# RMSNorm and matmul: half of the weights loaded ahead of x, and square roots for four tiles at a time

## The chip, the cores and the metric

The kernel runs on one core of one Trainium2 chip. The metric is the device time of one execution in microseconds (us); a median of several runs is given with its lowest and highest. A run has a state: "slow" where it is over 1.5% above the fastest of the same kernel, else "fast"; only fast runs are compared.

The engines: PE multiplies matrices, ACT (ScalarE), DVE (VectorE) and POOL (GpSimd) do the elementwise work, SP issues the transfers, and 16 DMA engines carry them. A transfer is split over the 16; I call the share that one engine has to carry its **ring**.

## The reference

```python
def reference(x, gamma, weight, eps):          # x 16 x 1024 x 512, weight 512 x 768, all float32
    rms = np.sqrt(np.mean(x ** 2, axis=-1, keepdims=True) + eps)
    x_norm = x / rms * gamma
    return np.matmul(x_norm, weight).astype(np.float32)
```

## The kernel before

The 16,384 rows are 128 tiles of 128 rows; two tiles are a pair. POOL casts a tile to bf16, PE transposes it (as 32-bit words, two bf16 each), DVE evacuates the transposes to SBUF, PE multiplies with the weights (four steps k, each 512 and 256 columns wide), and ACT and DVE alternate in scaling the result by 1/rms on its way to the output. ACT also squares x and sums the squares (`square`), and takes the root (`root`); DVE inverts it. Weights are scaled by gamma once and cast to bf16.

```python
    def root(i, n, ssq):
        rms = stats.tile([P, 4], F32, name="rms")
        nc.scalar.activation(out=rms[:, :n], in_=ssq[:, :n], func=AF.Sqrt, scale=1.0 / D, bias=eps_sb)
        rstd = stats.tile([P, 4], F32, name="rstd")
        nc.vector.reciprocal(out=rstd[:, :n], in_=rms[:, :n])
        ...
    def norms(i, n):
        ssq = stats.tile([P, 4], F32, name="ssq")
        for t in range(n):
            square(i + t, ssq[:, t:t + 1])
        root(i, n, ssq)
    ...
        touched = singles.tile([P, 2, 1], F32)
        nc.scalar.dma_start(out=touched, in_=wv[:, :, 0:1])      # one word of each weight row
        ...
        load_until(2)            # x tiles 0 and 1
        load_weights(0)          # weights for k = 0, 1
        load_until(3)            # x tile 2
        load_weights(1)          # weights for k = 2, 3
        load_until(2 * XG)       # x up to tile 31
        for _ in range(20):
            nc.sync.drain()
        ...
        warm_up(6)               # dummy matmuls, before the first data
        cast(0, nc.vector)
        square(0, ssq[:, 0:1])
        ...                      # gamma
        cast(1, nc.vector)
        square(1, ssq[:, 1:2])
        transpose_tile(0)
        warm_up(2)
        transpose_tile(1)
        warm_up(5)
        ...                      # weights 0 and 1 scaled, tiles 0 to 2 with k = 0, 1, then k = 2, 3
        for j in range(2, NP):
            load_until(2 * j + AHEAD)
            if j + 3 < NP:
                cast(2 * j + 6, nc.gpsimd, 2)
            if j + 1 < NP:
                norms(2 * j + 2, 2)
            ...                  # matmuls of pair j, transposes of a later pair in between
```

Outputs are stored eight tiles at a time in the middle, in smaller pieces at both ends; the last tile in two pieces (512 and 256 columns).

Of the kernel before, what the change touches and what calls it, by code (L numbers as in the profile page):

```python
# [12 lines left out]
F32 = mybir.dt.float32  # L13
# [5 lines left out]
def kernel(  # L19
# [8 lines left out]
    nc = tc.nc  # L28
    P = 128

    x = x.flatten_outer_dims()
    out = out.flatten_outer_dims()
# [4 lines left out]
    NP = NT // 2  # L37
# [27 lines left out]
    singles = ctx.enter_context(tc.tile_pool(name="singles", bufs=1))  # L65
# [3 lines left out]
    stats = ctx.enter_context(tc.tile_pool(name="stats", bufs=4))  # L69
# [2 lines left out]
    opsum = ctx.enter_context(tc.tile_pool(name="opsum", bufs=3, space=bass.MemoryType.PSUM))  # L72
    outp = ctx.enter_context(tc.tile_pool(name="out", bufs=3))

    x_tiles, xb_tiles, tp_tiles, rstd_of, xT_tiles, o_tiles = {}, {}, {}, {}, {}, {}

    def held(tiles, group, i, n=1):
        return tiles[i // group][:, i % group:i % group + n, :]

    def load(i):  # L80
        if i // XG not in x_tiles:
            x_tiles[i // XG] = xin.tile([P, XG, D], F32, name="xt")
        nc.sync.dma_start(out=held(x_tiles, XG, i, x_size[i]), in_=rows(x, i, x_size[i]))  # L83
# [3 lines left out]
    def load_until(i):  # L87
        while starts and starts[0] < i:
            load(starts.pop(0))

    def cast(i, engine, n=1):
        if i // 2 not in xb_tiles:
            xb_tiles[i // 2] = xbp.tile([P, 2, D], BF16, name="xb")
        engine.tensor_copy(out=xb_tiles[i // 2][:, i % 2:i % 2 + n, :], in_=held(x_tiles, XG, i, n))  # L94

    def square(i, ssq):
        jk = junk.tile([P, D], BF16, name="jk")
        nc.scalar.activation(out=jk, in_=held(x_tiles, XG, i)[:, 0, :], func=AF.Square, accum_out=ssq)  # L98
# [7 lines that stand above are left out]
            rstd_of[i + t] = rstd[:, t:t + 1]  # L106

    def norms(i, n):
        ssq = stats.tile([P, 4], F32, name="ssq")
        for t in range(n):  # L110
            square(i + t, ssq[:, t:t + 1])
        root(i, n, ssq)



    def transpose_word(j, t, h):
        if j not in tp_tiles:
            tp_tiles[j] = tpsum.tile([P, 2, 2, P], F32, name="tp")
        words = xb_tiles[j].rearrange("p a d -> p (a d)").bitcast(F32)
        lo = t * (D // 2) + h * P  # L120
        nc.tensor.transpose(out=tp_tiles[j][:, t, h, :], in_=words[:, lo:lo + P], identity=ident_f)  # L121

    def evac(j, t=0, n=2):
        if j not in xT_tiles:
            xT_tiles[j] = xt_pool.tile([P, 2, 2, P, 2], BF16, name="xT")
        src = tp_tiles.pop(j).rearrange("p t h m -> p t (h m)").bitcast(BF16)
        dst = xT_tiles[j].rearrange("p t h m c -> p t (h m c)")
        nc.vector.tensor_copy(out=dst[:, t:t + n, :], in_=src[:, t:t + n, :])  # L128


    def transpose_tile(i):
        for h in range(2):
            transpose_word(i // 2, i % 2, h)
        evac(i // 2, i % 2, 1)
# [7 lines left out]
    def accumulator():  # L142
        return opsum.tile([P, 2, WIDE], F32, name="ops").rearrange("p a b -> p (a b)")
# [16 lines left out]
    def matmuls(i, acc, ks, feed=None):  # L160
        for k in ks:
            matmul(i, k, acc, 0, WIDE)
            if feed:
                feed()
            matmul(i, k, acc, WIDE, O)
# [18 lines left out]
        return feed  # L184

    with tc.manual_schedule():

        wv = weight.rearrange("(h w c) o -> w h (c o)", w=P, c=2)
        touched = singles.tile([P, 2, 1], F32)
        nc.scalar.dma_start(out=touched, in_=wv[:, :, 0:1])  # L190
        g_row = singles.tile([2, P, 2], F32)
        nc.scalar.dma_start(out=g_row, in_=gamma.rearrange("(h w c) -> h w c", w=P, c=2))
        nc.scalar.preload_act_table(AF.Sqrt)  # L193
        w_f32 = singles.tile([P, K, O], F32)

        def load_weights(h):
            nc.sync.dma_start(out=w_f32[:, 2 * h:2 * h + 2, :].rearrange("p c o -> p (c o)"), in_=wv[:, h, :])  # L197

        load_until(2)
        load_weights(0)  # L200
        load_until(3)
        load_weights(1)
        load_until(2 * XG)

        for _ in range(20):
            nc.sync.drain()


        warm = singles.tile([P, WIDE], BF16)
        nc.vector.memset(warm, 0.0)  # L210
        eps_sb = singles.tile([P, 1], F32)
        nc.vector.memset(eps_sb, float(eps))  # L212
        ident_f = singles.tile([P, P], F32)
        make_identity(nc, ident_f)
        spare = accumulator()

        def warm_up(n):
            for _ in range(n):
                nc.tensor.matmul(out=spare[:, :WIDE], lhsT=warm[:, :P], rhs=warm, start=True, stop=True)  # L219

        w_bf = singles.tile([P, K, O], BF16)

        def weights(k, engine, lo=0, hi=O):
            scale(engine, w_bf[:, k, lo:hi], w_f32[:, k, lo:hi], g_sb[:, k % 2, k // 2:k // 2 + 1])


        ssq = stats.tile([P, 4], F32, name="ssq")
        warm_up(6)
        cast(0, nc.vector)
        square(0, ssq[:, 0:1])  # L230
        gp = tpsum.tile([P, 2, 2], F32, name="tp")
        for c in range(2):
            nc.tensor.transpose(out=gp[:, c, :], in_=g_row[:, :, c], identity=ident_f[:2, :2])  # L233
        g_sb = singles.tile([P, 2, 2], F32)
        nc.vector.tensor_copy(out=g_sb, in_=gp)  # L235
        cast(1, nc.vector)
        square(1, ssq[:, 1:2])
        transpose_tile(0)
        warm_up(2)
        transpose_tile(1)  # L240
        warm_up(5)
        acc = [accumulator() for _ in range(4)]
        weights(0, nc.vector, 0, WIDE)
        weights(0, nc.vector, WIDE, O)
        weights(1, nc.scalar)
        cast(2, nc.gpsimd)
        square(2, ssq[:, 2:3])
        matmuls(0, acc[0], [0, 1])
        transpose_tile(2)
        matmuls(1, acc[1], [0, 1])  # L250
        matmuls(2, acc[2], [0, 1])
        weights(2, nc.vector)
        root(0, 3, ssq)
        weights(3, nc.scalar)
        cast(3, nc.gpsimd)
        matmuls(0, acc[0], [2, 3])
        finish_tile(0, acc[0], nc.scalar)
        matmuls(1, acc[1], [2, 3])
        transpose_tile(3)
        finish_tile(1, acc[1], nc.vector)  # L260
        norms(3, 1)
        cast(4, nc.gpsimd)
        cast(5, nc.gpsimd)
        matmuls(2, acc[2], [2, 3])
        finish_tile(2, acc[2], nc.scalar)
        matmuls(3, acc[3], [0, 1, 2, 3], feeder([2], [0, 2, 2, 0], alone=True))
        finish_tile(3, acc[3], nc.vector)
        cast(6, nc.gpsimd, 2)
        cast(8, nc.gpsimd, 2)
        norms(4, 2)  # L270


        one, two, both = [1, 1, 0, 1, 1, 0, 0, 0], [1, 0, 1, 0, 1, 0, 1, 0], [1, 1, 1, 1, 1, 1, 1, 1]
        for j in range(2, NP):
            load_until(2 * j + AHEAD)
            if j + 3 < NP:
                cast(2 * j + 6, nc.gpsimd, 2)
            if j + 1 < NP:
                norms(2 * j + 2, 2)
            if j == NP - 1:  # L280
                break
            if j < 4:
                feed = feeder([j + 1], one)
            elif j == 4:
                feed = feeder([5, 6], both)
            elif j + 2 < NP:
                feed = feeder([j + 2], two)
            else:
                feed = None
            for i, engine in ((2 * j, nc.scalar), (2 * j + 1, nc.vector)):  # L290
                a = accumulator()
                matmuls(i, a, range(K), feed)
                finish_tile(i, a, engine)



        for i in (NT - 2, NT - 1):
            for lo, hi, engine in ((0, WIDE, nc.scalar), (WIDE, O, nc.vector)):
                a = accumulator()
                for k in range(K):  # L300
                    matmul(i, k, a, lo, hi)
                scale(engine, out_tile(i)[:, lo:hi], a[:, lo:hi], rstd_of[i])
                if i == NT - 1:
                    nc.sync.dma_start(out=rows(out, i, 1)[:, 0, lo:hi], in_=out_tile(i)[:, lo:hi])
            if i < NT - 1:
                store(i)
# [35 lines left out]
```

## Time and profile before

| | before |
|---|---|
| time, 3 runs | 211.19 us (211.04 to 211.26) |
| span of the profiled run | 209.6 us |
| second half of the weights lands | 11.45 us |
| first matmul on x | 9.55 us |
| PE starts tile 6 | 19.57 us |
| last output scale starts | 204.58 us |
| SP's last wait, for the stores | 2.7 us |

The last scale frees the last store, and SP waits until all stores have landed. The prediction shows the page, the chain of work and two stretches. Two further lines of the same page: PE's granted clock in the 40 slices (tenths of full speed), and the group of the roots (line, engine, operation, shapes, count, then busy us and mean ns, then idle time before).

```profile
PEclk9999999999999999999999999999999999999997
...
L102 ACT ACTIVATE rms<-ssq,eps_sb 128x2 f32<-128x2 f32 (+1 forms) x64 | 18.9, 296 | 2.1
```

64 roots take ACT 18.9 us.

### The profile page before, as it was taken

The page shows a single profiled execution, that of the slowest core. Times are in us where ns is not written, and L with a number is a line of the kernel's source. Part 1 is how long each engine was busy: PE and PEld are TensorE (multiplying, and loading weights), DVE is VectorE, ACT ScalarE, POOL GpSimd, SP SyncE. Part 2 cuts the span into 40 slices and gives each one's busy share as a digit, 9 for nine tenths or more (in the row PEclk, how much of TensorE's full clock was granted, in tenths as well). Part 3 has the DMA queues.
Part 4 walks back from the last instruction along what each step waited for, and adds up shares of the span by engine and source line. Part 5 has one row for each costly group of instructions (what it writes and reads, how often), then busy time and mean ns, then how long its engine had stood idle before and what let it go on. Part 6 is the DMA issues. An engine that isn't in the chain of part 4 may idle for free.

```text
span 209.6 us, 3586 instructions
## 1 busy us (share of the span) xinstructions
PE 199.2 (95%) x1270; PEld 137.7 (66%) x1295; DVE 111.5 (53%) x204; ACT 158.4 (76%) x388; POOL 65.8 (31%) x71
## 2 busy tenths in 40 slices
PE   7599999999999999999999999999999999999990
PEld 3256766677666776667766667666776666766650
DVE  2256566446545654564465456546645654565450
ACT  5279778877877787788778777877887787778750
POOL 1156533305323072313433044320732126330000
PEclk9999999999999999999999999999999999999997
DMA  6999999999999999999999999999999999799896
GB/s 207 364 431 421 432 399 441 416 391 444 427 444 422 430 427 430 449 417 421 416 450 438 416 433 427 436 435 407 441 427 433 430 433 425 310 399 422 347 383 236
DMA packets 7350, 85.69 MB, mean 409 GB/s; under 512 B 1058, under 2 KB 1188, under 8 KB 3748
## 3 DMA queue, kind: packets, MB, share of 16 engines
q1 hardware_dynamic: 7056, 85.46, 96.9%
q8 instruction: 10, 0.16, 0.3%
q14 instruction: 8, 0.07, 0.1%
q10 hardware_dynamic: 276, 0.00, 0.1%
HBM read 35.13 MB, written 50.33 MB: 408 GB/s over the span
## 4 chain that ended last, share of the span: by engine, by line
PE 88%; DMA 4%; ACT 3%; DVE 1%; issue 1%; SPq 1%
PE ops L156 75%; PE tp L121 13%; DMA w_f<-in_weight_dram 4%; ACT jk L98 1%; ACT ot L138 1%; SPq L83 1%; ACT rms L102 0%; DVE xT L128 0%; DVE w_bf L140 0%; DVE ot L140 0%; SPq L197 0%; DVE rstd L104 0%
## 5 line engine op out<-in xcount | busy, mean ns | idle before, releaser
L156 PE MATMUL ops<-w_bf,xT 128*128 128x512 bf16 (+1 forms) x999 | 192.8, 324 | 4.1 <-DVE w_bf L140 2.5
L156 PEld LDWEIGHTS <-xT 128*128 128x128 bf16 x1024 | 100.0, 98 | 59.3 <-issue 3.2
L94 POOL CAST xb<-xt 128x1024 bf16<-128x1024 f32 (+1 forms) x65 | 65.1, 1015 | 121.6 <-PE tp L121 68.0
L128 DVE COPY xT<-tp 128x1024 bf16<-128x1024 bf16 (+1 forms) x67 | 44.7, 667 | 82.1 <-PE tp L121 81.8
L138 ACT ACTIVATE ot<-ops,rstd 128x768 f32<-128x768 f32 (+1 forms) x65 | 58.1, 894 | 37.5 <-PE ops L156 36.7
L98 ACT ACTIVATE jk<-xt 128x512 bf16<-128x512 f32 x128 | 78.8, 619 | 0.5 <-DMA xt<-in_x_dram 0.5
L121 PE MATMUL tp<-ident_f,xb 128*128 128x128 f32 x256 | 69.2, 274 | 0.1
L140 DVE TENSOR_SCALAR ot<-ops,rstd 128x768 f32<-128x768 f32 (+1 forms) x65 | 64.5, 992 | 2.8 <-PE ops L156 2.8
L121 PEld LDWEIGHTS tp<-ident_f,xb 128*128 128x128 f32 x256 | 36.1, 142 | 3.7 <-PE tp L121 0.3
L98 ACT ACTIVATION_READ_ACCUMULATOR jk<-xt 128x1 f32 x128 | 24.4, 191 | 0.0
L102 ACT ACTIVATE rms<-ssq,eps_sb 128x2 f32<-128x2 f32 (+1 forms) x64 | 18.9, 296 | 2.1
L104 DVE RECIPROCAL rstd<-rms 128x2 f32<-128x2 f32 (+1 forms) x64 | 9.9, 155 | 2.1 <-ACT rms L102 2.0
L219 PE MATMUL ops<-warm 128*128 128x512 bf16 x13 | 5.0, 534 | 1.2 <-DVE eps_sb L212 1.2
L138 ACT ACTIVATE w_bf<-w_f,g_sb 128x768 bf16<-128x768 f32 x2 | 1.9, 935 | 4.6 <-DMA w_f<-in_weight_dram 4.6
L219 PEld LDWEIGHTS <-warm 128*128 128x128 bf16 x13 | 1.5, 124 | 2.7 <-DVE eps_sb L212 1.2
L140 DVE TENSOR_SCALAR w_bf<-w_f,g_sb 128x512 bf16<-128x512 f32 (+2 forms) x3 | 1.4, 485 | 2.9 <-DMA w_f<-in_weight_dram 2.9
L193 ACT ACT_TABLE_LOAD x1 | 1.3, 1283 | 1.8 <-issue 1.8
L94 DVE CAST xb<-xt 128x512 bf16<-128x512 f32 x2 | 0.8, 423 | 2.4 <-DMA xt<-in_x_dram 2.4
L233 PEld LDWEIGHTS tp<-ident_f,g_row 2*128 2x128 f32 x2 | 0.3, 202 | 0.8 <-issue 0.8
L210 DVE MEMSET warm<- 128x256 uint32 x1 | 0.3, 272 | 0.9 <-PEq L323 0.9
L233 PE MATMUL tp<-ident_f,g_row 2*128 2x2 f32 x2 | 0.4, 264 | 0.0
L235 DVE COPY g_sb<-tp 128x4 f32<-128x4 f32 x1 | 0.2, 163 | 0.3 <-PE tp L233 0.3
(7 smaller groups left out, 1.0 us busy)
## 6 DMA issues: line engine op xcount, KB each, us to landing
out_dram<-ot SPq DMA_DIRECT2D x12, 3072.0 KB, 16.1
xt<-in_x_dram SPq DMA_DIRECT2D x5, 4096.0 KB, 20.2
xt<-in_x_dram SPq DMA_DIRECT2D x3, 2048.0 KB, 18.0
out_dram<-ot SPq DMA_DIRECT2D x4, 1536.0 KB, 10.2
xt<-in_x_dram SPq DMA_DIRECT2D x4, 1024.0 KB, 13.2
out_dram<-ot SPq DMA_DIRECT2D x4, 768.0 KB, 9.1
out_dram<-ot SPq DMA_DIRECT2D x7, 384.0 KB, 10.1
w_f<-in_weight_dram SPq DMA_DIRECT2D x2, 768.0 KB, 8.1
```

The costliest lines, as they stand in the source:

```text
L83: nc.sync.dma_start(out=held(x_tiles, XG, i, x_size[i]), in_=rows(x, i, x_size[i]))
L94: engine.tensor_copy(out=xb_tiles[i // 2][:, i % 2:i % 2 + n, :], in_=held(x_tiles, XG, i, n))
L98: nc.scalar.activation(out=jk, in_=held(x_tiles, XG, i)[:, 0, :], func=AF.Square, accum_out=ssq)
L102: nc.scalar.activation(out=rms[:, :n], in_=ssq[:, :n], func=AF.Sqrt, scale=1.0 / D, bias=eps_sb)
L104: nc.vector.reciprocal(out=rstd[:, :n], in_=rms[:, :n])
L121: nc.tensor.transpose(out=tp_tiles[j][:, t, h, :], in_=words[:, lo:lo + P], identity=ident_f)
L128: nc.vector.tensor_copy(out=dst[:, t:t + n, :], in_=src[:, t:t + n, :])
L138: nc.scalar.mul(out=dst, in_=src, mul=r)
L140: nc.vector.tensor_single_scalar(out=dst, in_=src, scalar=r, op=mybir.AluOpType.mult)
L156: nc.tensor.matmul(out=acc[:, lo:hi], lhsT=xT_tiles[i // 2][:, i % 2, k // 2, :, k % 2], rhs=w_bf[:, k, lo:hi], start=(k == 0), stop=(k == ...
L193: nc.scalar.preload_act_table(AF.Sqrt)
L219: nc.tensor.matmul(out=spare[:, :WIDE], lhsT=warm[:, :P], rhs=warm, start=True, stop=True)
```

## The change

The intent is to have PE start on x earlier, by putting half of the weights first in the queue, and to take load off ACT and DVE by one root and one reciprocal for four tiles. The small read of one word per weight row goes, the casts of tiles 0 and 1 move from DVE to POOL, and seven dummy matmuls become three.

```diff
+    def norms_by_four(j):
+        if j % 2:
+            norm_sums[j] = stats.tile([P, 4], F32, name="ssq")
+        ssq = norm_sums[j - (j + 1) % 2]
+        for t in range(2):
+            square(2 * j + t, ssq[:, 2 * (1 - j % 2) + t:2 * (1 - j % 2) + t + 1])
+        if j % 2 == 0:
+            root(2 * j - 2, 4, ssq)
+        elif j == NP - 1:
+            root(2 * j, 2, ssq)
...
-        touched = singles.tile([P, 2, 1], F32)
-        nc.scalar.dma_start(out=touched, in_=wv[:, :, 0:1])
...
-        load_until(2)
         load_weights(0)
         load_until(3)
         load_weights(1)
...
         warm_up(6)
-        cast(0, nc.vector)
-        square(0, ssq[:, 0:1])
...
-        cast(1, nc.vector)
-        square(1, ssq[:, 1:2])
-        transpose_tile(0)
-        warm_up(2)
-        transpose_tile(1)
-        warm_up(5)
...
-        cast(2, nc.gpsimd)
-        square(2, ssq[:, 2:3])
+        warm_up(3)
+        for i in range(3):
+            cast(i, nc.gpsimd)
+            square(i, ssq[:, i:i + 1])
+        transpose_tile(0)
+        transpose_tile(1)
...
-            if j + 1 < NP:
+            if j < 4:
                 norms(2 * j + 2, 2)
+            for ahead in ([5, 6] if j == 4 else [j + 2] if 4 < j < NP - 2 else []):
+                norms_by_four(ahead)
```

More of the change, by code (lines that the diff above doesn't have):

```diff
@@ L73 @@
     outp = ctx.enter_context(tc.tile_pool(name="out", bufs=3))
-    x_tiles, xb_tiles, tp_tiles, rstd_of, xT_tiles, o_tiles = {}, {}, {}, {}, {}, {}
+    x_tiles, xb_tiles, tp_tiles, rstd_of, xT_tiles, o_tiles, norm_sums = {}, {}, {}, {}, {}, {}, {}
     def held(tiles, group, i, n=1):
@@ L186 @@
     with tc.manual_schedule():
-        wv = weight.rearrange("(h w c) o -> w h (c o)", w=P, c=2)
-        touched = singles.tile([P, 2, 1], F32)
-        nc.scalar.dma_start(out=touched, in_=wv[:, :, 0:1])
         g_row = singles.tile([2, P, 2], F32)
@@ L193 @@
         nc.scalar.preload_act_table(AF.Sqrt)
+        wv = weight.rearrange("(h w c) o -> w h (c o)", w=P, c=2)
         w_f32 = singles.tile([P, K, O], F32)
```

## The prediction

> **What bounds the kernel now.** I read the page first: busy shares, then the 40 slices, then the chain. After that I read the chain and the timeline of the first 20 us, the two stretches where the change acts, and POOL's waits in the middle.
>
> The page of the kernel before (busy time of each engine; then, in 40 slices of 5.24 us, PE and the DMA engines; then the chain that ended last):
>
> ```profile
> span 209.6 us, 3586 instructions
> PE 199.2 (95%) x1270; PEld 137.7 (66%) x1295; DVE 111.5 (53%) x204; ACT 158.4 (76%) x388; POOL 65.8 (31%) x71
> ...
> PE   7599999999999999999999999999999999999990
> ...
> DMA  6999999999999999999999999999999999799896
> ...
> PE ops L156 75%; PE tp L121 13%; DMA w_f<-in_weight_dram 4%; ACT jk L98 1%; ACT ot L138 1%; SPq L83 1%; ACT rms L102 0%; DVE xT L128 0%; DVE w_bf L140 0%; DVE ot L140 0%; SPq L197 0%; DVE rstd L104 0%
> ```
>
> TensorE is 9 in every slice but the first two and the last. 88% of the chain is its matmuls and transposes. DMA is also full, from slice 2 to slice 34. ACT is at 76% and on the chain only in the opening. So there are three parts: an opening, a long stretch that PE sets with DMA close behind it, and a tail.
>
> The chain in order of time shows the opening:
>
> ```profile
> 2.58 8.87 DMA w_f<-in_weight_dram
> 11.45 0.02 issue
> 11.47 0.63 DVE w_bf L140
> 12.11 0.04 issue
> 12.15 0.82 PE ops L156 x4
> 12.97 0.02 issue
> 13.00 0.90 ACT ot L138
> ...
> 18.43 0.30 ACT rms L102
> ...
> 18.76 0.04 DVE rstd L104
> 18.80 0.05 issue
> 18.84 0.68 DVE xT L128
> 19.52 0.05 issue
> 19.57 0.39 PE ops L156
> ```
>
> The second half of the weights is issued at 2.58 and lands at 11.45; that alone is the chain until then. ACT carries it from 13.00 to 18.73. From 19.57, where PE starts tile 6, the chain is PE. The period of one tile read off that chain (for example 26.58, 28.86, 30.38, 31.89) is 1.52 us. 122 tiles x 1.5185 us = 185.3, and 19.57 + 185.3 = 204.8; PE's last matmuls end at 204.56. So after 19.57 PE loses nothing. The last output scale and the last store then make 209.6, a tail of 5 us. **The change can alter the end only by moving the 19.57, or by putting a stall into the PE stretch.**
>
> DMA: a tile takes 256 KiB in and 384 KiB out, 655,360 bytes per 1.5185 us = 432 GB/s. The slices of the middle move 391 to 450, mostly 420 to 440. DMA is thus just at its limit at PE's pace. How much room there is shows in POOL's casts (start, time, idle before and what ended it):
>
> ```profile
> 123.31 3.99 POOL L94 CAST xb<-xt 128x1024 bf16<-128x1024 f32 x4 [8.25 <-DMA xt<-in_x_dram]
> 147.53 3.99 POOL L94 CAST xb<-xt 128x1024 bf16<-128x1024 f32 x4 [8.17 <-DMA xt<-in_x_dram]
> ```
>
> The load of tiles 80 to 95 lands at 123.31. Its first cast (1.04 us) ends at 124.35. PE transposes tile 80 while it computes tile 76, which starts at 19.57 + 70 x 1.5185 = 125.9. The room is some 1.6 us; the same sum for tile 96 gives 1.6. PE can't run more than about 1.6 us earlier unless these loads land earlier too.
>
> [...] most engines end the first half of the weights by 5.8 us, but four of the 16 stall for some 2.7 us at their first weight packets (single packets of 1.1 to 1.7 us against a median of 0.234 us, and pauses before them), so it lands only at 9.0. The same four are still behind at the second half, whose last packet ends at 11.05. [...] Here the first dummy matmuls come every 0.43 us and the last five in 1.24 us together, and 2.5 us of idle before the first real matmul at 9.55 didn't cool it. [...]
>
> **The change part by part.**
>
> (1) Order of the loads. Ahead of the end of the second half lie the same bytes as before: three x tiles (16 KiB per ring each) and two weight halves (48 KiB per ring each). From packets: 3 x 8 x 0.082 + 2 x 8 x 0.232 = 5.7 us per ring. Started at 1.75 that is 7.4; add a first-packet delay of 0.4, the four rings' stall of 2.7 and some 0.5 of smaller delays: 11.0, which is what was seen. Order alone doesn't change that sum. If the stall stays, the second half lands at 11.0 to 11.5 again: gain 0 to 0.4. If it goes (it came just as the small reads of one word per weight row, which are removed, had passed through the same rings, so they could be its cause), the gain is up to 2.7.
>
> (2) First matmul. Half 0 should land at 4.5 (no stall) to 7 (stall), x tile 0 0.7 later; then a POOL cast 0.62, transposes 0.43, evacuation 0.42: first matmul at 7 to 8.7 instead of 9.55. But PE had finished everything that half 0 allows, tiles 0 to 2 with k = 0 and 1, just before 12.15: it waited only some 0.25 us there. An earlier start without an earlier second half turns into waiting: gain at most 0.25.
>
> (3) The casts of tiles 0 and 1 go from DVE (0.42 us each) to POOL (0.62 us). Seven dummy matmuls become three. All lies before the second half lands: 0 on the path.
>
> (4) Roots by four. In the 57 pairs from tile 10 on, 62 roots over two become about 34 over four: some 28 ACTIVATEs of 0.296 = 8.3 us off ACT, 28 reciprocals of 0.155 = 4.3 us off DVE. ACT waits 36.7 us for PE in total, so this comes off idle time: 0. Squares come one pair (3.04 us) earlier and free x buffers earlier, but a load already queues behind issued stores (packets of the load issued at 54.29 start 4 us later), so landing isn't issue-bound: about 0.
>
> (5) A cost: at tile 8 the change puts four squares ahead of one root, to get two pairs ahead. ACT there before:
>
> ```profile
> 22.21 0.62 ACT L98 ACTIVATE jk<-xt 128x512 bf16<-128x512 f32 x1
> ...
> 23.57 0.30 ACT L102 ACTIVATE rms<-ssq,eps_sb 128x2 f32<-128x2 f32 x1
> 24.56 0.90 ACT L138 ACTIVATE ot<-ops,rstd 128x768 f32<-128x768 f32 x1 [0.69 <-PE ops L156]
> ```
>
> Four squares of 0.81 from 22.21 end at 25.45, the root at 25.78, the reciprocal at 25.95. DVE works in order, and in its order the evacuation of pair 5 stands behind that reciprocal: it moves from 24.45 to 25.97 and ends at 26.66. PE wants that pair for tile 10 at 26.1: a stall of about 0.6 us. Later pairs have nothing of the kind (odd ones have no root, even ones the old order).
>
> Sum: stall stays: 211.2 - 0.3 + 0.6 = 211.5. Stall goes: 211.2 - 2.6 + 0.6 = 209.2.
>
> **The rivals.** (a) The weight stall vanishes with the small reads: 209.2. For it: its timing. Against it: those reads look like a deliberate warm-up of the weights' addresses. (b) Without that warm-up, all 16 rings stall at the cold weights, and longer: half 2 lands perhaps 1 us later, 212.5. For it: first x packets also took 0.2 to 0.58 us instead of 0.08. [...] (d) PE starts earlier but x loads don't: stalls near 120 us and later give back all beyond 1.6 us: 210.2. (e) ACT is the true bound and the roots give back 8 us: against it, ACT's 36.7 us of waiting for PE and PE's gapless stretch; I give it 2%.
>
> **Range and chances.** I weigh "stall stays" 0.45, "goes, in whole or part" 0.35, "worse" 0.2: near 0.45 x 211.5 + 0.35 x 209.8 + 0.2 x 212.6 = 211.1. I say 211.0, range 208.9 to 212.9. Faster by over 2% needs 207.0, below even the best sum: 0.02. Slower by over 2% needs 215.4: 0.03.
>
> **What would show it.** The landing of the second half (11.45 before) and the start of tile 6 (19.57 before) should move by nearly the same amount, and the span with them, plus a gap of 0.6 us on PE before tile 10 with DVE's evacuation as its releaser. The PE stretch should keep 1.5185 us per tile; ACT's busy time should fall by some 8 us without effect. The prediction is wrong if PE shows gaps in the middle (DMA), if its clock drops in the opening, or if the period of a tile changes.

The forecast came to 0.45 x 211.5 + 0.35 x 209.8 + 0.2 x 212.6 = 211.1 and was put at 211.0. That the small reads are a warm-up, and that without them the second half lands 1 us later (rival b), were guesses that no trace shows; in e3, without the reads, it landed at 11.38. That DMA is at its limit is read from its share, 0.99 from 20 to 200 us.

## The result, and the profile after

The changed kernel took 210.83 us (210.49 to 211.55, six runs), the kernel before in the same rounds 211.12 us (210.89 to 211.67, six runs). The ratio of after to before is 0.9986, with a 95% interval of 0.9966 to 1.0007: the same, within 2%. A ratio is the mean time of one kernel's fast runs over the mean of the other's fast runs of the same rounds, so it isn't quite the ratio of the two medians.

The page after (the lines that answer to those of before):

```profile
span 209.2 us, 3496 instructions
PE 200.1 (96%) x1266; PEld 137.5 (66%) x1291; DVE 109.0 (52%) x173; ACT 149.5 (71%) x359; POOL 67.1 (32%) x73
...
PEclk9889999999999999999999999999999999999997
DMA  6999999999999999999999999999999999699886
...
PE ops L168 77%; PE tp L133 13%; DMA xt<-in_x_dram 3%; ACT jk L98 1%; ACT ot L150 1%; ACT rms L102 0%; SPq L83 0%; DVE xT L140 0%; POOL xb L94 0%; DVE ot L152 0%; SPq L206 0%; DVE rstd L104 0%
...
L102 ACT ACTIVATE rms<-ssq,eps_sb 128x4 f32<-128x4 f32 (+3 forms) x35 | 10.4, 297 | 1.1
```

ACT is busy 149.5 us instead of 158.4; 35 roots take 10.4 us. The chain has no weights any more: its DMA is now an x tile. And PE's clock has two digits of 8 near the start, where it had 9.

The chain of work in order of time, after (start, duration, what):

```profile
2.11 5.99 DMA xt<-in_x_dram
...
8.15 0.62 POOL xb L94
...
8.82 0.54 PE tp L133 x2
9.35 3.55 PE ops L168 x12
...
12.93 0.90 ACT ot L150
...
18.77 0.68 DVE xT L140
...
19.50 0.39 PE ops L168
```

x tile 2 lands at 8.10 and is now the last arrival that counts. The second half of the weights lands at 10.06, 1.4 us earlier than before, so the opening had that much to give. Yet the first output scale starts at 12.93 (13.00 before) and PE's tile 6 at 19.50 (19.57 before). From there 185.01 us lead to the last output scale at 204.51; before, 204.58 - 19.57 is 185.01 too.

What took the 1.4 us? The windows of the opening give a stretch, its length, then busy us (instructions) of PE, PEld, DVE, ACT and POOL, PE's granted clock, the DMA engines' busy share, and GB/s. First the kernel before, then the changed one:

```profile
5.60:9.03 3.43, 1.43 (x8) 0.67 (x7) 0.45 (x2) 0.03 (x1) 0.00 (x0) 1.00 0.94 347
9.03:12.44 3.41, 2.81 (x16) 1.44 (x16) 1.86 (x5) 2.75 (x5) 0.92 (x2) 1.00 1.05 431
```

```profile
5.60:9.03 3.43, 1.84 (x11) 0.93 (x11) 1.40 (x4) 2.76 (x8) 1.84 (x3) 1.00 1.02 393
9.03:12.44 3.41, 3.41 (x13) 1.66 (x12) 1.13 (x3) 1.14 (x2) 1.02 (x2) 0.50 1.04 429
```

From 9.03 to 12.44 the changed kernel has PE busy all the time, but at a clock of 0.50: 13 matmuls and transposes. (At full clock, e1 below has 21 in the same stretch.) PE's timeline after shows what that costs, and what PE did just before it:

```profile
6.67 0.44 PE L133 MATMUL tp<-ident_f,xb 128*128 128x128 f32 x2 [1.02 <-POOL xb L94]
7.31 0.44 PE L133 MATMUL tp<-ident_f,xb 128*128 128x128 f32 x2 [0.20 <-POOL xb L94]
7.63 0.82 PE L168 MATMUL ops<-w_bf,xT 128*128 128x512 bf16 x4
8.82 0.54 PE L133 MATMUL tp<-ident_f,xb 128*128 128x128 f32 x2 [0.37 <-POOL xb L94]
9.15 4.39 PE L168 MATMUL ops<-w_bf,xT 128*128 128x512 bf16 x16
```

The first matmul on x starts at 7.63, 1.9 us earlier than before. The next 16 need 4.39 us. In the stretch before the drop PE is idle for at most 1.02 us at a time, but apart from transposes it runs only 0.82 us of matmuls and the last 0.03 us of a dummy. The kernel before, whose clock stayed at 1.00, is idle for up to 2.52 us at a time in the same stretch, but has 1.36 us of matmuls other than transposes, all dummies.

### The profile page after: what moved, and what is told of

Its sections match the earlier page's. It is cut to its first block, busy times and chain, and to the rows that moved or that the text cites. A ratio compares the mean times of both kernels' runs of the same rounds, so it can differ in the third digit from the quotient of the medians.

```text
span 209.2 us, 3496 instructions
## 1 busy us (share of the span) xinstructions
PE 200.1 (96%) x1266; PEld 137.5 (66%) x1291; DVE 109.0 (52%) x173; ACT 149.5 (71%) x359; POOL 67.1 (32%) x73
## 4 chain that ended last, share of the span: by engine, by line
PE 90%; DMA 3%; ACT 3%; issue 1%; SPq 1%; DVE 1%; POOL 0%
PE ops L168 77%; PE tp L133 13%; DMA xt<-in_x_dram 3%; ACT jk L98 1%; ACT ot L150 1%; ACT rms L102 0%; SPq L83 0%; DVE xT L140 0%; POOL xb L94 0%; DVE ot L152 0%; SPq L206 0%; DVE rstd L104 0%
## 5 line engine op out<-in xcount | busy, mean ns | idle before, releaser
L94 POOL CAST xb<-xt 128x1024 bf16<-128x1024 f32 (+1 forms) x67 | 66.4, 1002 | 120.2 <-PE tp L133 75.2
L102 ACT ACTIVATE rms<-ssq,eps_sb 128x4 f32<-128x4 f32 (+3 forms) x35 | 10.4, 297 | 1.1
L104 DVE RECIPROCAL rstd<-rms 128x4 f32<-128x4 f32 (+3 forms) x35 | 5.8, 167 | 3.3 <-ACT rms L102 3.3
L227 PE MATMUL ops<-warm 128*128 128x512 bf16 x9 | 4.2, 628 | 1.2 <-DVE eps_sb L220 1.2
L227 PEld LDWEIGHTS <-warm 128*128 128x128 bf16 x9 | 1.0, 132 | 2.6 <-issue 1.4
```

Source lines behind the costliest of these rows:

```text
L94: engine.tensor_copy(out=xb_tiles[i // 2][:, i % 2:i % 2 + n, :], in_=held(x_tiles, XG, i, n))
L227: nc.tensor.matmul(out=spare[:, :WIDE], lhsT=warm[:, :P], rhs=warm, start=True, stop=True)
```

## The experiments

Twelve runs followed (e12 is the kernel of e3 once more). The table has them all: median and range of six runs, the ratio to the kernel before in the same rounds with its 95% interval, and from the profile the start of tile 6, the start of the last output scale, SP's last wait, and the span.

| kernel | us (lowest to highest) | ratio [95%] | tile 6 | last scale | SP wait | span |
|---|---|---|---|---|---|---|
| before | 211.12 (210.89 to 211.67) | | 19.57 | 204.58 | 2.7 | 209.6 |
| after | 210.83 (210.49 to 211.55) | 0.9986 [0.9966, 1.0007] | 19.50 | 204.51 | 2.4 | 209.2 |
| e1 | 210.96 (210.72 to 211.21) | 0.9979 [0.9948, 1.0010] | 18.17 | 203.18 | 3.6 | 209.1 |
| e2 | 211.04 (210.68 to 211.31) | 0.9983 [0.9949, 1.0017] | 18.97 | 203.98 | 2.6 | 208.9 |
| e3 (profile slow) | 213.05 (211.19 to 214.53) | 1.0052 [1.0003, 1.0101] | 19.49 | 204.50 | 5.6 | 212.7 |
| e4 | 210.84 (210.66 to 211.34) | 0.9977 [0.9945, 1.0009] | 18.04 | 203.05 | 3.5 | 208.8 |
| e5 (wrong result) | 209.38 (209.27 to 209.65) | 0.9906 [0.9873, 0.9939] | 17.91 | 202.93 | 2.3 | 207.5 |
| e6 (wrong result) | 210.20 (208.84 to 211.82) | 0.9946 [0.9901, 0.9991] | 17.60 | 202.61 | 2.1 | 207.1 |
| e7 | 214.66 (214.53 to 214.82) | 1.0154 [1.0120, 1.0187] | 17.98 | 203.79 | 5.5 | 212.8 |
| e8 (wrong result) | 210.48 (210.36 to 210.75) | 0.9956 [0.9926, 0.9987] | 18.08 | 203.09 | 3.5 | 208.9 |
| e9 | 210.84 (210.62 to 210.99) | 0.9974 [0.9943, 1.0005] | 18.02 | 203.04 | 3.6 | 209.1 |
| e10 | 212.92 (212.81 to 213.15) | 1.0074 [1.0045, 1.0102] | 18.38 | 203.39 | 5.3 | 211.0 |
| e11 | 211.16 (210.68 to 211.51) | 0.9984 [0.9948, 1.0021] | 18.22 | 203.23 | 4.0 | 209.7 |
| e12 (same kernel as e3) | 211.82 (210.72 to 212.84) | 1.0019 [0.9977, 1.0060] | 18.66 | 203.68 | 4.7 | 210.7 |

The kernel before took 211.09 to 211.14 us (medians) in the rounds of all of these, on three chips. Its row above is that of the result alone. In the rounds of the experiments, 10 of its 34 runs took over 212 us (eight fast ones, 212.14 to 212.85, and two slow ones). Of the 36 runs of the six right kernels with the weights first and no empty instructions added (after, e1, e2, e4, e9, e11), none took over 211.55. So the ratios of the experiments lie below those of the medians, and the new order may have removed the late runs; no experiment asks why.

### First round: what held the opening

My first theory was that the half clock ate the gain of the opening and that without it the kernel would be about 1.3 us faster. The rivals were that the roots matter, and that the small reads, not the order, caused the stall of the weights.

**e1: the changed kernel with eight dummy matmuls instead of three.**

```diff
-        warm_up(3)
+        warm_up(8)
```

> The changed kernel with eight dummy matmuls instead of three before the first transposes. In the changed kernel the clock was granted at half from 9.03 to 12.44 us. Theory (the cooled clock ate what the earlier weights gave): no half-clock window in the opening; 16 matmuls that took 4.39 us take about 3.0; tile 6 starts at about 18.1 instead of 19.50; span 209.2 -> about 207.9, time 0.994 of before. Rival (ACT or the x loads set the start of tile 6 anyway): the clock stays full but tile 6 starts at 19.2 to 19.5 and the time stays within 0.2 us of the changed kernel.

The clock stays at full. The windows of the opening in e1:

```profile
5.60:9.03 3.43, 2.60 (x14) 1.05 (x13) 1.37 (x4) 2.63 (x7) 1.86 (x3) 1.00 0.98 389
9.03:12.44 3.41, 3.37 (x21) 1.96 (x22) 1.13 (x3) 2.07 (x4) 1.00 (x2) 1.00 1.04 430
```

There are 21 matmuls and transposes instead of 13 in the same stretch, 16 matmuls take 3.01 us instead of 4.39, and tile 6 starts at 18.17, 1.33 us earlier than after. The last output scale starts 1.33 us earlier too, at 203.18. But the span is 209.1, not the expected 207.9, and the time 210.96: nothing of it arrives. SP's last wait grew from 2.4 to 3.6 us. So the clock was what held the opening, and it wasn't what sets the end.

**e2: the changed kernel with the roots of before.**

```diff
-            if j < 4:
+            if j + 1 < NP:
                 norms(2 * j + 2, 2)
-            for ahead in ([5, 6] if j == 4 else [j + 2] if 4 < j < NP - 2 else []):
-                norms_by_four(ahead)
```

> The changed kernel with the old roots (two tiles at a time, one pair ahead) throughout: the opening's change alone. Theory (ACT is idle in the PE stretch, roots cost nothing): same as the changed kernel within 0.2 us; ACT busy back up by about 8 us. Rival (roots by four carry the small gain, or the four squares in a row at tile 8 cost something): 0.3 us or more slower, or 0.3 us or more faster, than the changed kernel.

211.04 against 210.83 us for the changed kernel, ratios to the kernel before of 0.9983 and 0.9986. The roots by four are worth nothing that these runs can see, and PE's stretch from tile 6 to the last output scale is 185.01 us with either. (The clock dropped here as well, but from 7.64 to 11.06, so tile 6 started at 18.97.)

**e3: the kernel before without the small reads of the weights.**

```diff
-        touched = singles.tile([P, 2, 1], F32)
-        nc.scalar.dma_start(out=touched, in_=wv[:, :, 0:1])
```

> The kernel before without the small read of one word per weight row. Theory (those small reads caused the stall of four rings at the weights): first half of the weights lands at about 6.3 instead of 9.0, second half at about 8.8 to 9.5 instead of 11.45, tile 6 starts 1.4 us or more earlier, span about 208. Rival (the stall belongs to the first reading of the weights when x comes ahead; the small reads are a warm-up that helps or does nothing): landings at 9.0 and 11.4 or later, span 209.6 or more.

The halves of the weights land at 8.81 and 11.38, as with the small reads (8.91 and 11.45). So the small reads don't cause the stall. Its runs spread from 211.19 to 214.53 and the profiled one is a slow one, so its time is not used; e12 repeats it.

**e4: the changed kernel with the small reads put back.**

```diff
+        touched = singles.tile([P, 2, 1], F32)
+        nc.scalar.dma_start(out=touched, in_=wv[:, :, 0:1])
         g_row = singles.tile([2, P, 2], F32)
```

> The changed kernel with the small read of one word per weight row put back on the ACT queue ahead of gamma. Theory (small reads cause the stall): second half lands at 11 or later instead of 10.08, four rings lag by about 2.5 us. Rival (order of the loads removed the stall): landings unchanged at 5.4 and 10.1, time unchanged within 0.2 us.

The halves land at 5.26 and 9.80 (5.29 and 10.06 without the reads). e3 and e4 together: with x first the stall is there with the reads and without; with the weights first it is gone, or nearly, with and without. So it goes with the order and not with the reads; its size varies from run to run (e12 below has 10.55). PE's clock happened to stay full here, and tile 6 started at 18.04; the time, 210.84, is still that of the changed kernel.

### Second round: where the earlier PE stretch ends up

e1 and e4 finish the computing 1.3 to 1.5 us earlier than the changed kernel and end hardly earlier (209.1 and 208.8 against 209.2). The new theory: the last bytes of one or a few DMA rings, which carry a backlog, set the end. Its rival: the tail after the last scale is some fixed work that grew for another reason. The windows of the last microseconds show the rings. One ring of 16 is a DMA share of 0.06 (1/16 = 0.0625). The columns are as above: clock, DMA share and GB/s are the last three. First before, then after, then e1:

```profile
206.00:207.00 1.00, 0.00 (x0) 0.00 (x0) 0.00 (x0) 0.00 (x0) 0.00 (x0) 1.00 0.97 379
207.00:208.00 1.00, 0.00 (x0) 0.00 (x0) 0.00 (x0) 0.00 (x0) 0.00 (x0) 0.50 0.52 185
```

```profile
207.00:208.00 1.00, 0.00 (x0) 0.00 (x0) 0.00 (x0) 0.00 (x0) 0.00 (x0) 0.50 0.42 144
```

```profile
206.00:207.00 1.00, 0.00 (x0) 0.00 (x0) 0.00 (x0) 0.00 (x0) 0.00 (x0) 0.79 0.20 75
207.00:208.00 1.00, 0.00 (x0) 0.00 (x0) 0.00 (x0) 0.00 (x0) 0.00 (x0) 0.50 0.08 29
```

In the kernel before all 16 rings work until 207 and half of their time to 208. In e1 most are done by 206, as the earlier PE lets them; on average some three are at work from 206 to 207 and little more than one from 207 to 208. The store has landed only when that one has.

The times at which the 16 rings report the last store say the same:

```text
             8th of 16    16th of 16    between
before        207.80        208.51       0.71
after         207.72        208.22       0.50
e1            206.39        208.13       1.74
e5            206.12        206.56       0.44
e7            206.99        211.79       4.80
e10           206.70        210.04       3.34
e12           206.88        209.71       2.83
```

Before, after and e1 end within 0.4 us of each other at the slowest ring (208.51, 208.22 and 208.13), though the eighth ring of e1 is 1.3 to 1.4 us ahead. In all fourteen profiles the eighth ring reports 3.2 to 3.3 us after the last output scale starts, and the span ends 0.9 to 1.1 us after the slowest ring's report. So most rings follow PE, and what differs between the tails is the lag of the slowest ring, from 0.3 (e6) to 4.8 us (e7).

Stores of the middle show it as well: the store issued near 170 us lands at 186.15 in the kernel before and in e1, although it was issued 1.4 us earlier in e1. Its eighth ring reports at 181.85 before and at 181.30 in e1. So a ring is over 4 us behind in the middle even in the kernel before, and makes most of it up by the end. The next kernels try it out: take bytes off the rings, or put some on.

**e5: e1 without the store of tiles 48 to 55 (that part of the result is wrong).**

```diff
-        if i == first + n - 1:
+        if i == first + n - 1 and first != 48:
```

> Wrong result on purpose: e1_warm without the store of tiles 48 to 55 (3 MB, some 7.3 us of all DMA engines). In e1_warm PE ended 1.3 us earlier than in the changed kernel, but the last store landed at 208.13 as in both kernels (208.2, 208.22), its slowest ring 1.74 us behind the median. Theory (the slowest ring's backlog, never idle, sets a floor of about 208.1 for the last landing): with 7 us less work the backlog is gone, the last store lands about 2.4 us after its issue, at 206.3 to 206.7; span 207.2 to 207.7, that is 1.4 to 1.9 us under e1_warm. Rival (the tail after PE is longer in e1_warm for another reason, for example a slower store): span stays at 208.8 to 209.2.

209.38 us, a ratio of 0.9906. The last scale starts at 202.93, only 0.25 us earlier than in e1, but the span is 1.6 us shorter. The windows of e5 have the rings empty by 207:

```profile
206.00:207.00 1.00, 0.00 (x0) 0.00 (x0) 0.00 (x0) 0.00 (x0) 0.00 (x0) 1.00 0.01 5
```

With 3 MB less to move, the slowest ring lags by only 0.44 us, and the end follows PE: 207.5 - 202.93 is a tail of 4.6 us, where e1 had 5.9.

**e6: the changed kernel without the same store (wrong).**

> Wrong result on purpose: the changed kernel, nothing else altered, without the same store. Theory: here PE's end (204.5) and the ring floor nearly coincide, so only the 0.5 us lag of the slowest ring goes: span 208.5 to 208.8, 0.3 to 0.7 us under the changed kernel where its clock was halved. Rival (DMA alone is the bound and PE has slack): span falls by more than 1.5 us.

The edit is that of e5. The runs spread from 208.84 to 211.82, and in the profiled one the clock stayed full, so the case that I had set up, a late PE with free rings, is not what ran. (x tile 2 came earlier than in the profile of the changed kernel: PE transposed it at 8.28 instead of 8.82, and matmuls followed sooner.) That one profile is like e5: the last scale at 202.61 and a tail of 4.5 us. The spread I can't explain, and I draw nothing more from it.

**e7: e1 with 60 empty SP instructions after each store of eight tiles.** They do nothing, but they are fetched: the page lists fetches of instructions among the DMA queues, with their share of the 16 engines' time (7 on q14 in e1).

```diff
             nc.sync.dma_start(out=rows(out, first, n), in_=held(o_tiles, OG, first, n))
+            for _ in range(60 if n == OG else 0):
+                nc.sync.drain()
```

> e1_warm with 60 empty waits of the SP queue after each store of eight tiles: some 800 more instructions on an engine that is idle, so more instruction fetches on the DMA rings, no other work. Theory (the rings that also fetch instructions are the slow ones, each fetch of 0.3 to 1 us putting its ring behind by 0.4 to 1.4 us): 6 to 8 more fetches, the last store's slowest ring 1 to 4 us later, span 210 to 213, PE's end unchanged. Rival (fetches are spread over the rings or hidden): span within 0.3 us of e1_warm.

The 0.3 to 1 us of a fetch are in the packet records: in the kernel before, those of 8 KB take 0.31 to 0.54 us within the span, those of 16 KB 0.88 to 1.10. The 6 to 8 fetches are an estimate that the page after gives too: 17 fetches with 0.22 MB for 3,496 instructions are 63 bytes each, so 800 more are six fetches of 8 KB. The 0.4 to 1.4 us by which a fetch puts its ring behind is an estimate too, near the fetch and the longer packet behind it: in the kernel after, a packet of 24 KB that starts as a fetch ends takes 1.08 to 1.39 us, against a median of 0.912. What came was 0.74 us for each added fetch in e7 and 0.65 in e10.

214.66 us, 3.70 more than e1. The page's line of the fetches, and the windows of the end, in e7:

```profile
q14 instruction: 12, 0.10, 0.1%
```

```profile
208.00:209.00 1.00, 0.00 (x0) 0.00 (x0) 0.00 (x0) 0.00 (x0) 0.00 (x0) 0.50 0.06 25
209.00:210.00 1.00, 0.00 (x0) 0.00 (x0) 0.00 (x0) 0.00 (x0) 0.00 (x0) 0.50 0.07 28
210.00:211.00 1.00, 0.00 (x0) 0.00 (x0) 0.00 (x0) 0.00 (x0) 0.00 (x0) 0.50 0.07 26
```

Five more fetches than e1 (12 against 7), of 8 KB each, and from about 208.3 to 211.8 exactly one ring is at work while 15 have finished. PE's last scale is 0.61 us later than in e1 (203.79; PE waits 0.58 us for a cast before 174.26), but the eighth ring, which follows PE, reports at 206.99: the end is set by the one ring at 211.79.

**e10: e1 with 30 empty instructions per store instead of 60.** It checks that the effect goes by the fetch.

> As e7_warm_drains (e1_warm plus 60 empty waits per large store, 12 fetches of 8 KB instead of 7, last landing 3.66 us later), with 30 per store. Theory (about 0.7 us per added fetch on the slowest ring): 2 to 3 more fetches than e1_warm, 1.4 to 2.2 us longer than e1_warm: 212.3 to 213.2. Rival (the empty waits delay the issue of loads or stores, not the rings): the time doesn't follow the count of fetches; half as many waits cost far less than half, or nothing.

10 fetches, 3 more than e1; 212.92 us, 1.96 more. That is 0.65 us per fetch, where e7 had 0.74. The last scale is only 0.21 us later than in e1, so PE can't be the cause. A fetch itself takes 0.31 us in most packet records. In e7, the packets of 24 KB that start as the fetches at 77, 102, 126 and 151 us end (e1 has none at these times) take 1.21 to 1.23 us, against a median of 0.91. Together that is some 0.6 us, most of this cost; after other fetches the packet is 0.1 to 0.4 us longer. (The records don't name the ring; that such a packet is on the fetch's ring is read from its start.) This leaves one reservation: the empty instructions also keep SP from issuing for a moment, and no run separates that from the fetches. But the last stores go out at 203.67 in e10 and 203.46 in e1, and the end differs by 1.9 us. And e7 issues a store at 168.68, 0.19 us before e1 does: its eighth ring reports at 181.48 (181.30 in e1), its slowest at 189.09 (186.15). The store isn't late; one ring is.

**e9: e1 without the 20 empty instructions that the kernel has from the start.** If a fetch went with them, some 0.7 us should go.

```diff
-        for _ in range(20):
-            nc.sync.drain()
```

> e1_warm without the 20 empty waits that the SP queue has after its first loads: fewer instructions. Theory (each fetch of instructions puts one DMA ring behind, and the slowest ring sets the end): if one of the seven 8 KB fetches of e1_warm goes, 0.3 to 0.7 us faster than e1_warm; if none goes, the same within 0.2 us. Rival (those waits are there to delay something in the opening): slower than e1_warm by more than 0.3 us.

210.84 us, ratio 0.9974; the trace still has 7 fetches on that queue. No fetch was saved, so the kernel doesn't tell whether one less helps.

**e8 and e11: e1 with the first 16 tiles stored in two large pieces instead of many small ones**, to have fewer packets on the rings. In the packet records of the kernel before, a ring's 24 KB of one tile take 0.912 us in one packet (median), 4 x 0.234 in packets of 6 KB, and 8 x 0.121 = 0.968 in packets of 3 KB.

```diff
-    o_first, o_size = stretches(OG, {0: opening, 1: [4, 4], last - 1: [4, 4], last: [2, 2, 1, 1, 1, 1]})
+    o_first, o_size = stretches(OG, {last - 1: [4, 4], last: [2, 2, 1, 1, 1, 1]})
```

> e1_warm with the first 16 tiles stored in two stores of eight tiles in place of eight smaller ones; packets of 24 KB instead of 3 to 12 KB, which save some 0.03 us a tile per ring. Theory (ring floor): 0.2 to 0.4 us faster than e1_warm. Rival (opening stores must start early to keep the rings full): a gap in the DMA share before 30 us, and a slower kernel.

210.48 us, ratio 0.9956, but the result is wrong, by my mistake: the rows of the first tiles were loaded in one order and stored in another. e11 repairs it by removing the `if i < XG` branch of `rows`, so that all rows have one order.

> e8_warm_big_stores gave a wrong result, since its first 16 tiles were loaded in one order of rows and stored in another. Here all tiles use the row order of the later ones (a partition holds 16 consecutive rows), so the loads keep their packet sizes and the two large stores are right. Theory (ring floor, fewer and larger packets): correct, 0.2 to 0.5 us faster than e1_warm (210.96), near 210.5. Rival (strided reads in the opening are slower): weights and x land later, 211 or more.

211.16 us, ratio 0.9984, and correct. The gain of e8 didn't come back; the slowest ring ended at 208.61, later than in e1. The two intervals overlap, so whether row order matters stays open. The expectation of a gain was wrong.

**e12: the kernel of e3 once more.**

> e3_before_no_touch once more, unaltered: its six times spread from 211.2 to 214.5 us and its profiled run had one ring 4 us behind at the end. If the missing small reads cause that: 212 to 214 again. If it was chance of that hour: 211.0 to 211.6, as the kernel before.

This time the profile is a fast run, if one of the longer ones (212.48 us), and it is the plainest case against the old idea of the end. The weights land at 7.98 and 10.55 (the stall is there, but smaller), tile 6 starts at 18.66, 0.9 us earlier than in the kernel before, the last scale at 203.68, also 0.9 earlier, and yet the span is 210.7, 1.1 us longer. The windows of the end in e12:

```profile
208.00:209.00 1.00, 0.00 (x0) 0.00 (x0) 0.00 (x0) 0.00 (x0) 0.00 (x0) 0.50 0.09 33
209.00:210.00 1.00, 0.00 (x0) 0.00 (x0) 0.00 (x0) 0.00 (x0) 0.00 (x0) 0.50 0.02 6
```

One or two rings run until 209.7. Why they lag from run to run I can't say. That the missing reads cause it is not shown: the kernel before has the same spread in the same rounds (210.76 to 212.85 in fast runs, here 210.72 to 212.84).

No kernel with a right result is clearly faster than both: e1, e4 and e9 stand at 0.9974 to 0.9979, and all their intervals hold 1.

## Why the prediction was right or wrong

The number, 211.0 us against 210.83, was right, but by luck: it is a weighted mean of cases none of which came as a whole. The loads gained 1.4 us and the halved clock took 1.33 us of it back; the stall of 0.6 us that was added didn't come; and e1 shows that without the halved clock the end would not have moved either. By the prediction's own signs its account failed: the landing moved by 1.4 us and tile 6 by 0.07, and the clock dropped in the opening.

- **PE's stretch: right.** 185.01 us from tile 6 to the last output scale before, after and in e1, no gap, the same period per tile.
- **The loads (step 1): the better case came, in part.** Stall or no stall were the two cases for the second half: 11.0 to 11.5, or a gain of up to 2.7 us. It landed at 10.06, a gain of 1.4. The cause that I suspected, the small reads, is refuted by e3 and e4; the stall goes with the order. The prediction's "order alone doesn't change that sum" added up the bytes and took the stall as a constant beside them. For most rings the sum held: the eighth ring reports the second half at 8.83 before and 8.54 after, and only the slowest moved, from 11.45 to 10.06. (The prediction's "four of the 16" is three and a milder fourth: the last reports of the first half come at 6.93, 8.30, 8.85 and 8.91, and the packets of 1.1 to 1.7 us are three.) Why rings stall at weights that are queued behind x stays open.
- **The first matmul (step 2):** predicted at 7 to 8.7, measured 7.63. The conclusion, that its own gain is small without an earlier second half, was not put to the test: the second half came 1.4 us earlier, and the chain ran through x tile 2 and the matmuls behind it.
- **The clock: it dropped.** At 0.50 from 9.03 to 12.44 it lost 1.33 us at tile 6 (19.50 against e1's 18.17), which cancelled the loads' 1.4. The prediction names a drop as a sign against itself, weighed as part of "worse" only. What makes the clock drop is not shown. In the 3.4 us before the drop, matmuls other than transposes made up 0.85 us here and 0.81 us in e2; in the kernel before they made up 1.36 us from 5.60 to 9.03, and there the clock stayed full.
- **The stall of 0.6 us at tile 10 (step 5): absent.** ACT and then DVE after the change, at that place:

```profile
22.14 0.62 ACT L98 ACTIVATE jk<-xt 128x512 bf16<-128x512 f32 x1
22.66 0.19 ACT L98 ACTIVATION_READ_ACCUMULATOR jk<-xt 128x1 f32 x1
22.75 0.62 ACT L98 ACTIVATE jk<-xt 128x512 bf16<-128x512 f32 x1
...
24.72 0.30 ACT L102 ACTIVATE rms<-ssq,eps_sb 128x4 f32<-128x4 f32 x1
```

```profile
25.14 0.66 DVE L140 COPY xT<-tp 128x1024 bf16<-128x1024 bf16 x1
```

  A square starts 0.61 us after the one before it, not 0.81: the read of the accumulator overlaps the next square in part, and I had added the two durations. Four squares end near 24.6 instead of 25.45, the root starts at 24.72, and the evacuation ends at 25.80, ahead of PE's need at about 26.1. (DVE did keep its order, as the prediction says: idle for 1.28 us until the root, it took the reciprocal at 25.05 and then the evacuation at 25.14, though the pair's last transpose had ended at 24.34.) Starts in a timeline, not durations, give the pace.
- **The roots (step 4): right.** ACT's busy time fell by 8.9 us (some 8 predicted) and DVE's reciprocals from 9.9 to 5.8 us, and e2 shows that it does nothing to the time. (The counts were off: the pairs from tile 10 on are 59, not 57, and the roots went from 64 to 35 in all. The difference, 29 instead of 28, hardly matters.)
- **The step that failed** is the sentence "The change can alter the end only by moving the 19.57, or by putting a stall into the PE stretch", with "a tail of 5 us" as a constant. The tail was 5.0 us before, 4.7 after, 5.9 in e1, 4.6 in e5, 7.0 in e12 and 9.0 in e7. The end is the later of two: PE's last scale plus some 4.5 us (e5 and e6, where hardly anything lags), and the slowest ring's report, at 208.1 to 208.5 in before, after and e1 alike, plus some 1.0 us. In the kernel before the two stood within half a microsecond of each other (209.1 and 209.6), so the chain showed PE alone. The prediction's "stall goes" sum, 209.2, could not have come true even at full clock: e1 is that case, and it took 210.96.
- **Rival (d), DMA gives the gain back, was right in kind and wrong in place.** I looked for it at the x loads near 120 us, and for PE gaps. e1, 1.4 us ahead of before, has no such gap: PE's waits there are all in the opening. The giving back is at the last stores, where PE no longer waits and so no engine shows it. The DMA rows of the page say "full", as an average over 16 rings (0.99 from 20 to 200 us); from 180 to 202.5 us the share is below 1 (0.86 to 0.90 in before, after and e1) and still single rings are behind.

What is shown and what is argued: e5 shows that fewer bytes end the lag, e7 and e10 that the traffic of a few more fetches lengthens it on one ring, and the windows and reports show how many rings are late. That the slowest ring ends at a fixed time because it has its bytes to carry and no pause is the reading that fits these, and is argued, not shown; I did not measure every ring's pauses. Open are: the stall of the weights, the makeup of the lag that e1 has without extra fetches, the spread of e3 and e12, and that of e6.

## What to carry to other kernels

Where DMA is full beside the engine that bounds (here a share of 0.99 from 20 to 200 us, with PE busy for 178.7 of the 180), the end can be the later of the engine's last result and the slowest DMA ring; look at the last microseconds in 1 us windows, and count rings by sixteenths of the DMA share, before you count a gain of the opening as a gain at the end. Dummy matmuls that look idle can carry the clock over the wait for the first data (with eight it stayed at 1.00; with three it was 0.50 for some 3.4 us after the change and in e2, though full in e4 and e6): take them away only with the granted clock of the opening in view. And check a right number by its steps: here a gain and a loss in the opening cancelled, and neither would have reached the end.
